# Start of a block feed-forward: filter transform ahead of the operands, first weight sums ahead of the norm, modulation rows spread out, a third residual row buffer

## The chip, the cores and the metric

One core of a Trainium2 chip runs the whole program. Its engines each work through their own list of instructions in order: PE (TensorE, matrix products), DVE (VectorE, elementwise work on two operands), ACT (ScalarE, copies, casts and functions), POOL (GpSimd, elementwise) and SP (SyncE, which here issues every transfer). An instruction that must wait for another engine waits on a semaphore, and everything behind it on its own engine waits with it. The metric is the time of one execution in device microseconds (us); the median over runs counts.

## What is computed

Two layers of a diffusion backbone over 512 latent and 256 context tokens of width 1024 (768 tokens, kept as columns). Layer 0 mixes with a gated DeltaNet and banded attention, layer 1 with retention and a Hyena convolution. Each layer ends in a modulated SwiGLU feed-forward. In the reference:

```
x = x + mod[2] * (o_lat.astype(x.dtype) @ w_out)
x = x + mod[5] * swiglu(modulate(rmsnorm(x, norm_ffn_w[layer]), mod[3], mod[4]),
                        ffn_w_in[layer], ffn_w_out[layer])
...
def swiglu(h, w_in, w_out):
    gate, up = jnp.split(h @ w_in, 2, axis=-1)
    return (jax.nn.silu(gate) * up) @ w_out
...
c_act = jax.nn.silu(c)
mod = jnp.split((c_act @ mod_w[layer] + mod_b[layer])[:, None], 6, axis=-1)
```

The context tokens have modulation values of their own (`mod_c`, from `c_ctx`), and the Hyena part needs the Fourier transform of its filters, which depends on the weights alone. Both are side work that this kernel fits in around layer 0's feed-forward.

## The kernel before

**The feed-forward of layer 0.** `block_ffn` computes gate and up of one hidden block of 128 channels together, as a 2 by 2 block product: the two halves are the halves of the 1024 input channels on one side and the two halves of 384 tokens on the other. Seven products do the work of eight. Each product is 12 matmuls of 128x384: four blocks of 128 input channels, and three terms for each (both numbers are split into a high and a low part: high by high, high by low, low by high). There are 22 hidden blocks ("pairs" of a gate and an up weight below, numbered from 0), worked through in groups of 4, 4, 4, 4, 3 and 3. After a group's hidden blocks, `group_out` multiplies them by the output weight for each of the 8 blocks `d` of 128 output channels and adds the product to a row of the residual: it loads the row `xr` (384 KB) from DRAM, adds on DVE, and stores it again.

**Operands.** Before the first product, `block_operands` makes the seven activations from the residual `xt` and the norm's statistics: 16 DVE instructions (SCALAR_TENSOR_TENSOR, with the statistics in PSUM) and as many ACT instructions apply scale and shift; then for each part an ACT cast gives the high part (`hx`, `x`, `t7h`) and a DVE subtraction the low part (`hx`, `x`, `t7l`), and further DVE additions and subtractions form the sums (tiles `hhi`, `hlo`, `hxt2`).

**Weights.** `weights(j)` inside `block_ffn` loads gate and up of a pair (two `wr` tiles of 512 KB), splits the gate tile by an ACT cast and a DVE subtraction (`wh`, `wl`; products 1 and 2), forms four sums on DVE (`us`, and one in place in `wr`) and splits five units (`uh` on ACT, `ul` on DVE; products 6, 7, 5, 4, 3 in this order).

**The side work.** `hy_freq` transforms the filters: 16 matmuls of `hs` by `F`, ACT copies `he` out of PSUM, and POOL adds and subtracts two at a time into `hab` (four tiles, two POOL instructions each), which SP stores to `hD`. It is written behind `block_operands`. `mod_rows` computes 56 blocks of modulation values on DVE, as a task in pieces: its first piece loads the vector `cb` (1 MB) and the first weight row `wm` (512 KB); its second applies silu to `cb` on ACT; and each piece from there on loads the next `wm` and runs one or two DVE instructions `wj` (the 24 blocks that the context needs have two). `K.bg(n, "mod")` runs n pieces where it stands; `BLOCK_MOD` says how many follow each hidden block, and `group_out` runs one for each `d`.

**What sets the order.** A scheduler reorders the program's instructions within each engine, and tiles come from pools that reuse memory. All transfers lie on one queue, SP's, and are issued in its order. `cb` lies in memory that `hab` had held, so its load waits for the last store of `hab`, on SP's queue and for the data.

```
BLOCK_MOD = (2,) * 6 + (1,) * 8 + (0,) * 8
...
            ops = K.block_operands(xt, st, saf, sbf, hp)
            K.hy_freq(*pf, 0, hsD, hD)
```

Of the kernel before, what the change touches and what calls it, by code (L numbers as in the profile page):

```python
# [10 lines left out]
F32R = mybir.dt.float32r  # L11
# [8 lines left out]
P = 128  # L20
D = 1024
KD = D // P
NL = 512
NC = 256
NT = NL + NC
# [9 lines left out]
FFN_GROUPS = (8, 7, 7)  # L35
BLOCK_GROUPS = (4, 4, 4, 4, 3, 3)
BLOCK_HID = 6
BLOCK_MOD = (2,) * 6 + (1,) * 8 + (0,) * 8
V_EARLY = (1,)
INV_PACE = (6, 6, 10, 5, 24)  # L40
SCAN_ORDER = "ssss" + "sa" * 7 + "as" + "aoaoaao"
# [110 lines left out]
class Kern:  # L152
# [1130 lines left out]
                split(n, k, xp[d + k][:, c:c + h])  # L1283
        return ops

    def block_ffn(self, l, ops, hp, hq, xr):
        K, A = self, self.A
        h = HT

        def unit(src, n=4):  # L1290
            hi, lo = (K.t(hq, (P, 4, P), "u" + x, F32R, bufs=6)[:, :n] for x in "hl")
            A.copy(out=hi, in_=src)  # L1292
            K.sub(lo, src, hi)
            return hi, lo

        def weights(j):
            g, u = (K.t(K.wp, (P, KD, P), "wr", bufs=3) for _ in range(2))
            K.dma(g, K.I["ffi"][l, j, 0])
            K.dma(u, K.I["ffi"][l, j, 1])
            hi, lo = (K.t(K.wp, (P, KD, P), n, F32R, bufs=2) for n in ("wh", "wl"))  # L1300
            A.copy(out=hi, in_=g)
            K.sub(lo, g, hi)
            S = K.t(hq, (P, 12, P), "us", bufs=1)
            s1, s2, s3 = S[:, :4], S[:, 4:8], S[:, 8:]
            K.add(s1, u[:, :4], u[:, 4:])
            K.sub(s2, s1, g[:, :4])
            K.sub(s3, g[:, :4], u[:, :4])
            K.sub(u[:, :4], g[:, 4:], s2)
            w = {1: (hi[:, :4], lo[:, :4]), 2: (hi[:, 4:], lo[:, 4:])}
            for m, src in ((6, s2), (7, s3), (5, s1), (4, u[:, 4:]), (3, u[:, :4])):  # L1310
                w[m] = unit(src)
            return w

        def product(ps, w, m, first=False):
# [5 lines left out]
        def hidden(j):  # L1320
            w = weights(j)
            x, y, z = K.mmps()[:, :h], K.wkps()[:, :h], K.wkps()[:, :h]
            f = K.t(hq, (P, 2 * h), "hf", bufs=2)
            a, b = (K.t(hq, (P, h), c, bufs=2) for c in ("ha", "hb"))
            product(x, w, 1, True)
            A.copy(out=f[:, :h], in_=x)
            product(y, w, 2, True)
            K.add(f[:, :h], y, f[:, :h])
            K.act(f[:, :h], f[:, :h], AF.Silu)
            product(x, w, 6)  # L1330
            A.copy(out=a, in_=x)
            product(z, w, 7, True)
            product(x, w, 5)
            A.copy(out=b, in_=x)
            K.add(b, z, b)
            product(z, w, 4)
            K.add(a, z, a)
            K.mul(f[:, :h], f[:, :h], a)
            product(x, w, 3)
            K.act(f[:, h:], x, AF.Silu)  # L1340
            K.mul(f[:, h:], f[:, h:], b)
            hi, lo = (K.t(hp, (P, NT), t, F32R, bufs=BLOCK_HID) for t in ("hhi", "hlo"))
            A.copy(out=hi, in_=f)
            K.sub(lo, f, hi)
            return hi, lo

        xt = None

        def group_out(g0, hs):
            nonlocal xt  # L1350
            nh = len(hs)
            last = g0 + nh == NH
            if last:
                xt = K.t(K.bp, (P, KD, NT), "x", bufs=1)
            for d in range(KD):
                raw = K.t(K.wp, (P, KD, P), "wr", bufs=3)[:, :nh]
                K.dma(raw, K.I["ffo"][l, d][:, g0:g0 + nh, :])
                w = unit(raw, nh)
                x = xt[:, d] if last else K.t(hq, (P, NT), "xr", bufs=2)
                K.dma(x, xr[d])  # L1360
                pl, pc = K.mmps(), K.wkps()
                K.proj_fm(w, ([t[0] for t in hs], [t[1] for t in hs]), K.halves(pl, pc))
                for p, c, r in K.parts(pl, pc):
                    K.stt(x[:, c], p, K.modc[l][:, 40 + d, r:r + 1], x[:, c])
                if not last:
                    K.dma(xr[d], x)
                K.bg(1, "mod")

        pend, start = [], 0
        for gn in BLOCK_GROUPS:  # L1370
# [448 lines left out]
def body(ctx, tc, I, out, dbg=None, stop=None):  # L1819
    K = Kern(ctx, tc, I, out, dbg)  # L1820
    K.setup()
    hD = K.t(K.dp, [2, 2, P, 2, 2, 512], "hD")
    hsD = K.t(K.dp, [2, 4, P, 2, 512], "hsD")
# [8 lines left out]
    with ExitStack() as s:  # L1832
        with ExitStack() as s2:
# [3 lines left out]
            xt = K.t(K.bp, (P, KD, NT), "x", bufs=1)  # L1837
# [16 lines left out]
        pf = K.pool(s, "hyf0")  # L1854
# [18 lines left out]
    with ExitStack() as s:  # L1873
        hp = K.pool(s, "hp")
        with ExitStack() as s2:
            K.sp = K.sx = K.pool(s2, "sp1", side="right")
            pf = [K.pool(s2, "hyf1a"), K.pool(s2, "hyf1b", side="right")]
            st = K.norm_stats(xt)
            for d in range(KD):
                K.dma(xr[d], xt[:, d])  # L1880
            ops = K.block_operands(xt, st, saf, sbf, hp)
            K.hy_freq(*pf, 0, hsD, hD)
        hq, mp = K.pool(s, "hq"), K.pool(s, "mp1", side="right")
        K.tasks["mod"] = [K.mod_rows(mp, [(0, n, True) for n in range(40, 48)] + [(1, n, n < 16) for n in range(48)])]
        xt = K.block_ffn(0, ops, hp, hq, xr)
    if stop == "l0":
        K.dma(dbg["x"], xt)
        return
# [41 lines left out]
```

## Time and profile before

| | |
|---|---|
| median of 3 runs | 1882.78 us (1876.31 to 1886.25) |
| the profiled execution | 1874.94 us |
| its span, first to last instruction | 1873.2 us |
| mean granted TensorE clock | 0.969 |
| PE busy | 1763.2 us, 94% of the span |
| DVE busy | 1192.3 us, 64% |
| ACT busy | 686.6 us, 37% |
| POOL busy | 105.7 us, 6% |

Times inside a run are counted from the start of the span. The granted clock is TensorE's, as a share of 2.4 GHz; 0.50 is its lower level, 1.2 GHz. An arrow `a <- b` behind "idle" or in a wait says that `a` stood still until `b` was done.

### The profile page before, as it was taken

What the parts mean: (1) busy time and instruction counts of PE and PEld (TensorE: products, weight loads), DVE (VectorE), ACT (ScalarE), POOL (GpSimd) and SP (SyncE); (2) the same over time, 40 slices, a digit from 0 to 9 for tenths busy, and PEclk for the clock granted to TensorE, in tenths of its full rate; (3) what the DMA queues carried; (4) which work ended last, traced back from release to release, by engine and by line L of the source; (5) the groups of instructions that cost most, each with busy time, mean ns of one, the idle gap of its engine ahead of it and who ended that gap; (6) DMA issues with size and microseconds to landing.
All of it is one profiled execution on the core that took longest, in us unless ns stands there. A gap on an engine that the chain in (4) does not pass through costs nothing.

```text
span 1873.2 us, 28543 instructions
## 1 busy us (share of the span) xinstructions
PE 1763.2 (94%) x11047; PEld 1596.8 (85%) x11047; DVE 1192.3 (64%) x2423; ACT 686.6 (37%) x1417; POOL 105.7 (6%) x94
## 2 busy tenths in 40 slices
PE   5999999999898399999999998999999999999999
PEld 4988899988696399999999997687998888888887
DVE  5686696458747799988765557668645663333333
ACT  2444444145615342433333323422442432222221
POOL 0011001100002300000000000200003100000000
PEclk9999999779899699999999998999999999999999
DMA  8344465445383447687744356422443523333332
GB/s 330 112 152 134 123 215 178 101 155 180 96 267 127 152 133 229 205 277 249 224 146 139 114 187 240 168 96 94 127 136 102 185 75 101 92 100 96 96 97 95
DMA packets 123076, 286.71 MB, mean 153 GB/s; under 512 B 28729, under 2 KB 45545, under 8 KB 119228
## 3 DMA queue, kind: packets, MB, share of 16 engines
q1 hardware_dynamic: 122940, 284.88, 46.5%
q8 instruction: 87, 1.43, 0.3%
q14 instruction: 49, 0.40, 0.1%
HBM read 228.96 MB, written 55.87 MB: 152 GB/s over the span
## 4 chain that ended last, share of the span: by engine, by line
PE 77%; DVE 10%; DMA 5%; ACT 3%; issue 3%; POOL 1%; SPq 0%; POOLq 0%; DVEq 0%; ACTq 0%
PE mm L193 52%; PE wk L193 23%; PE wk L197 1%; PE sa L193 1%; DVE wl L200 1%; POOL hab L200 1%; DVE ac L213 1%; DMA wm<-in_modt_dram 1%; ACT wh L250 1%; DMA xr<-xr 1%; PE sa L197 1%; DVE wj L213 0%; DMA rvt<-rvD 0%; DMA x<-in_xall_dram 0%; DMA vD<-tk 0%
## 5 line engine op out<-in xcount | busy, mean ns | idle before, releaser
L193 PE MATMUL mm<-hx,wh 128*128 128x512 f32 (+2 forms) x1968 | 524.3, 361 | 8.1 <-ACT hx L408 3.6
L193 PEld LDWEIGHTS mm<-hx,wh 128*128 128x128 f32 x1968 | 356.9, 190 | 52.0 <-ACT hx L408 3.8
L193 PE MATMUL mm<-hx,wl 128*128 128x512 f32 (+2 forms) x984 | 327.1, 360 | 0.8 <-DVE wl L200 0.8
L200 DVE TENSOR_TENSOR wl<-wr,wh 128x1024 fp32r<-128x1024 f32 (+1 forms) x159 | 193.3, 1216 | 190.5 <-ACT wh L250 179.1
L250 ACT CAST wh<-wr 128x1024 fp32r<-128x1024 f32 (+1 forms) x137 | 142.7, 1041 | 419.0 <-PE mm L193 414.0
L193 PE MATMUL mm<-wh,hx 128*128 128x256 f32 x1216 | 231.8, 290 | 2.6 <-DVE sv L963 1.1
L193 PEld LDWEIGHTS mm<-hx,wl 128*128 128x128 f32 x984 | 183.8, 190 | 24.0 <-issue 3.9
L193 PEld LDWEIGHTS mm<-wh,hx 128*128 128x128 f32 x1216 | 193.7, 195 | 5.5 <-issue 1.7
L193 PE MATMUL mm<-wl,hx 128*128 128x256 f32 x608 | 175.3, 289 | 0.0
L193 PE MATMUL mm<-hx,uh 128*128 128x384 f32 x352 | 90.4, 338 | 32.4 <-ACT uh L1292 32.4
L193 PEld LDWEIGHTS mm<-wl,hx 128*128 128x128 f32 x608 | 118.2, 195 | 1.0 <-issue 0.6
L213 DVE SCALAR_TENSOR_TENSOR wj<-wm,cb 128x1024 bf16<-128x1024 f32 x80 | 97.6, 1220 | 21.3 <-ACT cb L221 13.9
L1292 ACT CAST uh<-wr 128x512 fp32r<-128x512 f32 (+1 forms) x92 | 55.1, 602 | 148.5 <-PE wk L193 84.8
L213 DVE SCALAR_TENSOR_TENSOR x<-mm,modc,x 128x256 f32<-128x256 f32 (+3 forms) x72 | 40.7, 585 | 90.8 <-PE mm L193 88.6
L193 PEld LDWEIGHTS mm<-hx,uh 128*128 128x128 f32 x352 | 64.2, 190 | 32.8 <-ACT uh L1292 32.7
L200 DVE TENSOR_TENSOR ul<-wr,uh 128x512 fp32r<-128x512 f32 (+1 forms) x92 | 60.8, 664 | 20.4 <-ACT uh L1292 20.2
L193 PE MATMUL mm<-hhi,wh 128*128 128x512 f32 x176 | 68.5, 389 | 0.0
L193 PE MATMUL mm<-hhi,wl 128*128 128x512 f32 x176 | 68.5, 389 | 0.0
L193 PE MATMUL mm<-hlo,wh 128*128 128x512 f32 x176 | 68.5, 389 | 0.0
L1292 ACT CAST uh<-us 128x512 fp32r<-128x512 f32 x66 | 39.4, 620 | 77.4 <-DVE us L200 32.8
L200 DVE TENSOR_TENSOR hf<-hf,mm 128x512 f32<-128x512 f32 x22 | 15.1, 687 | 71.6 <-PE mm L193 71.6
L193 PE MATMUL mm<-hx,ul 128*128 128x384 f32 x176 | 59.3, 337 | 0.0
(438 smaller groups left out, 3441.9 us busy)
## 6 DMA issues: line engine op xcount, KB each, us to landing
wr<-in_ffi_dram SPq DMA_DIRECT2D x88, 512.0 KB
xr<-xr SPq DMA_DIRECT2D x80, 384.0 KB
wm<-in_modt_dram SPq DMA_DIRECT2D x56, 512.0 KB
wm<-in_modw_dram SPq DMA_DIRECT2D x20, 1024.0 KB
wr<-in_ffo_dram SPq DMA_DIRECT2D x32, 256.0 KB
wr<-in_rett_dram SPq DMA_DIRECT2D x16, 512.0 KB
wr<-in_ffo_dram SPq DMA_DIRECT2D x16, 448.0 KB
wr<-in_abf_dram SPq DMA_DIRECT2D x12, 512.0 KB
```

The lines of the kernel that those rows point to most:

```text
L193: self.T.matmul(out=out, lhsT=l, rhs=r, start=start, stop=stop, skip_group_check=True)
L197: self.T.transpose(out, in_, self.ident[:n, :n])
L200: (eng or self.V).tensor_tensor(out=out, in0=a, in1=b, op=op)
L213: self.V.scalar_tensor_tensor(out=out, in0=a, scalar=s, in1=b, op0=op0, op1=op1, **kw)
L250: self.A.copy(out=hi, in_=raw)
L1292: A.copy(out=hi, in_=src)
```

## The change

Four edits. `hy_freq` is written ahead of `block_operands`. The first pair's loads, its four sums and the split of four of its units are written ahead of the norm (`block_first`, `block_sums`), where products 6 and 7 take their weights from one cast of two units at once, and the sum for product 5 is copied into the gate's tile, so that only three casts `uh` are left for `weights(0)`. The modulation pieces are spread over all 22 hidden blocks, with one for every second `d` of `group_out`. The row `xr` has three buffers, and `ha` and `hb` one each where they had two.

```diff
-BLOCK_MOD = (2,) * 6 + (1,) * 8 + (0,) * 8
+BLOCK_MOD = (0, 1, 2, 2, 2, 2) + (1,) * 4 + (2,) * 12
+BLOCK_ROWS = 3
...
+    def block_sums(self, l, j, pool):
+        K = self
+        g, u = (K.t(K.wp, (P, KD, P), "wr", bufs=3) for _ in range(2))
+        K.dma(g, K.I["ffi"][l, j, 0])
+        K.dma(u, K.I["ffi"][l, j, 1])
+        hi, lo = (K.t(K.wp, (P, KD, P), n, F32R, bufs=2) for n in ("wh", "wl"))
+        K.A.copy(out=hi, in_=g)
+        K.sub(lo, g, hi)
+        S = K.t(pool, (P, 12, P), "us", bufs=1)
+        s2, s3, s1 = S[:, :4], S[:, 4:8], S[:, 8:]
+        K.add(s1, u[:, :4], u[:, 4:])
+        K.sub(s2, s1, g[:, :4])
+        K.sub(s3, g[:, :4], u[:, :4])
+        K.sub(u[:, :4], g[:, 4:], s2)
+        return {1: (hi[:, :4], lo[:, :4]), 2: (hi[:, 4:], lo[:, 4:])}, {6: s2, 7: s3, 5: s1, 4: u[:, 4:], 3: u[:, :4]}, S, g
+
+    def block_first(self, l, pool):
+        K = self
+        w, src, S, g = K.block_sums(l, 0, pool)
+        hi, lo = (K.t(K.wp, (P, KD, P), n, F32R, bufs=2) for n in ("wh", "wl"))
+        K.A.copy(out=hi, in_=S[:, :8])
+        K.sub(lo, S[:, :8], hi)
+        w[6], w[7] = ((hi[:, i:i + 4], lo[:, i:i + 4]) for i in (0, 4))
+        K.A.copy(out=g[:, :4], in_=src[5])
+        return w, {5: g[:, :4], 4: src[4], 3: src[3]}
+
...
         def weights(j):
-            g, u = (K.t(K.wp, (P, KD, P), "wr", bufs=3) for _ in range(2))
...
-            for m, src in ((6, s2), (7, s3), (5, s1), (4, u[:, 4:]), (3, u[:, :4])):
-                w[m] = unit(src)
+            w, src = K.block_sums(l, j, hq)[:2] if j else first
+            for m in (6, 7, 5, 4, 3):
+                if m in src:
+                    w[m] = unit(src[m])
             return w
...
-            a, b = (K.t(hq, (P, h), c, bufs=2) for c in ("ha", "hb"))
+            a, b = (K.t(hq, (P, h), c, bufs=1) for c in ("ha", "hb"))
...
-                x = xt[:, d] if last else K.t(hq, (P, NT), "xr", bufs=2)
+                x = xt[:, d] if last else K.t(hq, (P, NT), "xr", bufs=BLOCK_ROWS)
...
-                K.bg(1, "mod")
+                K.bg(d % 2, "mod")
...
+            first = K.block_first(0, K.sx)
             st = K.norm_stats(xt)
...
+            K.hy_freq(*pf, 0, hsD, hD)
             ops = K.block_operands(xt, st, saf, sbf, hp)
-            K.hy_freq(*pf, 0, hsD, hD)
```

The names in the rows below end in a number of the tile and one of its allocation. On ACT, at the start of the operands (`hhi`, `hlo`: scale and shift; `hx`: high parts; `he`: filter copies), before:

```order
L1500 COPY he_1037_6442<-wk_1039_6447 128x512
L221 ACTIVATE hlo_1014_6301<-hlo_1014_6301,modc0_9_87 128x512
L221 ACTIVATE hlo_1014_6301<-hlo_1014_6301,modc0_9_87 128x256
L1259 CAST hx_1017_6304<-hlo_1014_6301 128x384
L221 ACTIVATE hhi_1011_6298<-hhi_1011_6298,modc0_9_87 128x512
L221 ACTIVATE hhi_1011_6298<-hhi_1011_6298,modc0_9_87 128x256
L1259 CAST hx_1017_6304<-hhi_1011_6298 128x384
L1500 COPY he_1041_6455<-wk_1042_6456 128x512
```

and of the change, some rows earlier in the same stretch:

```order
L1516 COPY he_1029_6350<-wk_1031_6355 128x512
L222 ACTIVATE hlo_1042_6381<-hlo_1042_6381,modc0_9_87 128x512
L222 ACTIVATE hlo_1042_6381<-hlo_1042_6381,modc0_9_87 128x256
L1516 COPY he_1033_6363<-wk_1034_6364 128x512
L1260 CAST hx_1045_6384<-hlo_1042_6381 128x384
L222 ACTIVATE hhi_1039_6378<-hhi_1039_6378,modc0_9_87 128x512
L222 ACTIVATE hhi_1039_6378<-hhi_1039_6378,modc0_9_87 128x256
L1516 COPY he_1033_6363<-wk_1035_6368 128x512
L1260 CAST hx_1045_6384<-hhi_1039_6378 128x384
```

The last copy `he` of the four pairs (`he_1033` in the change) now stands in front of the fifth of the eight `hx` casts shown here; before (`he_1045`, not shown) it stood behind all eight, behind the eight `x` casts and behind two of the four `t7h` casts.

On ACT at the end of the operands (`cb`: silu of the modulation vector, `hf`, `ha`, `hb`: product results copied out of PSUM), before:

```order
L1326 COPY hf_1095_6674<-mm_1092_6671 128x384
L221 ACT_TABLE_LOAD
L221 ACTIVATE cb_1072_6627<-cb_1072_6627 128x2048
L1292 CAST uh_1054_6503<-us_1053_6498 128x512
L1292 CAST uh_1056_6507<-us_1053_6498 128x512
L1292 CAST uh_1058_6511<-us_1053_6498 128x512
```

and of the change:

```order
L1319 CAST uh_1056_6508<-wr_995_6230 128x512
L1319 CAST uh_1058_6512<-wr_996_6231 128x512
L1319 CAST uh_1060_6516<-wr_996_6231 128x512
L1260 CAST t7h_1049_6388<-hlo_1040_6379 128x384
L1342 COPY hf_1065_6523<-mm_1062_6520 128x384
L1293 CAST wh_1072_6628<-wr_1070_6624 128x1024
L222 ACT_TABLE_LOAD
L222 ACTIVATE cb_1093_6761<-cb_1093_6761 128x2048
L1347 COPY ha_1066_6524<-mm_1062_6520 128x384
```

The casts `uh` stood behind the silu of `cb` and now stand ahead of it; what stands behind it now is the copy `ha`, of the result of product 6.

On PE behind products 1 and 2 of pair 0 (operands `t7h`, `t7l` belong to product 7, `hx_1047` and `hx_1048` of the change to products 6 and 5), before:

```order
L193 MATMUL wk_1065_6524<-hx_1017_6304,wl_1052_6495 128x384
L193 MATMUL mm_1092_6671<-hx_1017_6304,wl_1080_6643 128x384
L193 MATMUL mm_1064_6523<-hx_1019_6306,uh_1054_6503 128x384
L193 MATMUL mm_1064_6523<-hx_1020_6307,uh_1054_6503 128x384
L193 MATMUL wk_1066_6525<-t7h_1021_6308,uh_1056_6507 128x384
```

and of the change, around the end of product 7:

```order
L194 MATMUL wk_1064_6522<-t7l_1050_6389,wh_1000_6243 128x384
L194 MATMUL wk_1064_6522<-t7h_1049_6388,wl_1001_6244 128x384
L194 MATMUL mm_1085_6657<-hx_1045_6384,wh_1072_6628 128x384
L194 MATMUL mm_1085_6657<-hx_1046_6385,wh_1072_6628 128x384
L194 MATMUL wk_1086_6658<-hx_1045_6384,wh_1072_6628 128x384
L194 MATMUL wk_1086_6658<-hx_1046_6385,wh_1072_6628 128x384
L194 MATMUL mm_1062_6520<-hx_1047_6386,uh_1056_6508 128x384
```

Before, the first matmul behind products 1 and 2 needs a unit `uh` that stands behind the silu of `cb` on ACT. In the change products 7 and 6 (24 matmuls, with weights `wh_1000` and `wl_1001` made ahead of the norm) come first, and the first matmul with an `uh` is that of product 5; it writes over the result that `ha` copies. Product 1 of pair 1 (`mm_1092` before), which ran ahead of the wait, is `mm_1085` and comes behind.

## Rows read from the trace of the kernel before

**Rows 1.** Costliest groups of the page: busy us, mean ns, idle before and releaser.

```profile
L193 PE MATMUL mm<-hx,uh 128*128 128x384 f32 x352 | 90.4, 338 | 32.4 <-ACT uh L1292 32.4
...
L250 ACT CAST wh<-wr 128x1024 fp32r<-128x1024 f32 (+1 forms) x137 | 142.7, 1041 | 419.0 <-PE mm L193 414.0
```

**Rows 2.** Windows: us, busy PE, PEld, DVE, ACT, POOL, granted clock, DMA share, GB/s.

```profile
605.05:637.41 32.36, 0.00 (x0) 0.00 (x0) 18.49 (x37) 12.19 (x24) 21.53 (x4) 0.58 0.29 120
637.41:640.80 3.39, 3.39 (x11) 3.15 (x12) 3.39 (x7) 2.46 (x5) 0.00 (x0) 0.52 0.43 171
640.80:651.77 10.97, 10.97 (x64) 10.67 (x63) 10.97 (x20) 5.10 (x9) 0.00 (x0) 1.00 0.53 160
```

**Rows 3.** Chain that ends at 642 us: start, us, what.

```profile
589.79 1.12 ACT hhi L221 x2
590.91 0.40 ACT hx L1259
...
594.16 0.48 ACT he L1500
...
601.99 9.80 POOL hab L200
...
622.43 4.16 POOL hab L200 x3
626.60 2.60 DMA hD<-hab
...
629.33 4.23 DMA cb<-in_crow_dram
...
633.65 1.28 ACT L221
634.94 1.91 ACT cb L221
```

**Rows 4.** POOL in order of time: start, us, instruction, idle before.

```profile
594.72 2.50 POOL L200 TENSOR_TENSOR hab<-he 128x512 f32<-128x512 f32 x2 [7.18 <-ACT he L1500]
601.99 24.59 POOL L200 TENSOR_TENSOR hab<-he 128x512 f32<-128x512 f32 x4 [4.76 <-issue]
```

**Rows 5.** DVE in order of time: start, us, instruction (rows between left out).

```profile
594.76 1.13 DVE L213 SCALAR_TENSOR_TENSOR hhi<-x,saffn,mm 128x512 f32<-128x512 f32 x2
596.10 1.54 DVE L200 TENSOR_TENSOR hx<-hlo,hx 128x384 fp32r<-128x384 f32 x1 [0.20 <-ACT hx L1259]
...
601.65 0.55 DVE L200 TENSOR_TENSOR hx<-hlo,hx 128x384 fp32r<-128x384 f32 x1
602.12 0.55 DVE L200 TENSOR_TENSOR hhi<-hhi 128x384 f32<-128x384 f32 x1
...
619.45 0.69 DVE L200 TENSOR_TENSOR us<-wr 128x512 f32<-128x512 f32 x1
...
621.26 0.55 DVE L200 TENSOR_TENSOR hf<-wk,hf 128x384 f32<-128x384 f32 x1
```

**Rows 6.** Waits from 640 to 1140 us: engine, line, what for, us, times, longest.

```profile
DVE xr L213 <- DMA xr<-xr: 18.8, 13, 3.6
DVE wj L213 <- DMA wm<-in_modt_dram: 7.2, 11, 1.4
PE wk L193 <- DVE hb L200: 5.1, 3, 2.7
PE mm L193 <- ACT hb L1334: 1.0, 1, 1.0
```

**Rows 7.** Tile wj from 640 to 1140 us (ns min/median/max, first and last start).

```profile
L213 DVE SCALAR_TENSOR_TENSOR wj<-wm,cb x79: 1214/1219/1227, 641.0 to 916.2; 128x1024 bf16<-128x1024 f32 x79
```

**Rows 8.** Windows in the feed-forward, columns as in group 2.

```profile
857.00:868.00 11.00, 8.31 (x41) 7.75 (x41) 9.99 (x18) 1.66 (x5) 0.00 (x0) 0.91 0.75 283
640.00:720.00 80.00, 80.00 (x455) 78.70 (x454) 79.26 (x137) 35.89 (x64) 0.00 (x0) 1.00 0.48 146
950.00:1150.00 200.00, 200.00 (x1141) 196.91 (x1139) 122.46 (x217) 71.86 (x121) 0.00 (x0) 1.00 0.47 154
```

More of the change, by code (lines that the diff above doesn't have):

```diff
@@ L1284, in block_operands, with block_ffn @@
         return ops
-    def block_ffn(self, l, ops, hp, hq, xr):
+    def block_sums(self, l, j, pool):
[22 more added lines that the diff above has]
+        return w, {5: g[:, :4], 4: src[4], 3: src[3]}
+    def block_ffn(self, l, first, ops, hp, hq, xr):
         K, A = self, self.A
@@ L1296, in weights @@
         def weights(j):
-            g, u = (K.t(K.wp, (P, KD, P), "wr", bufs=3) for _ in range(2))
[L1298 to L1309, printed above, removed]
-            for m, src in ((6, s2), (7, s3), (5, s1), (4, u[:, 4:]), (3, u[:, :4])):
-                w[m] = unit(src)
+            w, src = K.block_sums(l, j, hq)[:2] if j else first
+            for m in (6, 7, 5, 4, 3):
+                if m in src:
+                    w[m] = unit(src[m])
             return w
@@ L1880, in body @@
                 K.dma(xr[d], xt[:, d])
+            K.hy_freq(*pf, 0, hsD, hD)
             ops = K.block_operands(xt, st, saf, sbf, hp)
-            K.hy_freq(*pf, 0, hsD, hD)
         hq, mp = K.pool(s, "hq"), K.pool(s, "mp1", side="right")
         K.tasks["mod"] = [K.mod_rows(mp, [(0, n, True) for n in range(40, 48)] + [(1, n, n < 16) for n in range(48)])]
-        xt = K.block_ffn(0, ops, hp, hq, xr)
+        xt = K.block_ffn(0, first, ops, hp, hq, xr)
     if stop == "l0":
```

## The prediction

> **What bounds the kernel now.** The page says that PE is busy for 94% of the span, so only what PE waits for can be won without doing less on PE. The first view is the list of costliest groups: one group of matmuls, `mm<-hx,uh`, has 32.4 us of idle time ahead of it, put down to the ACT cast `uh` [rows 1]. The windows place it at 605.05 to 637.41 us, the start of the feed-forward: PE does nothing there, and the 11 matmuls behind it take 3.39 us at a granted clock of 0.52, where the next 64 take 10.97 us at 1.00 [rows 2]. So a matmul takes 0.17 us at full clock and a product of twelve 2.1 us; the low clock costs another 1.5 us.
>
> The chain of waits that ends there says why. ACT was not slow: `uh` stands behind the silu of `cb`, `cb` behind its transfer, that behind the store of `hab`, and that behind POOL [rows 3]. POOL is the surprise: four additions `hab` from 601.99 took 24.59 us, though the pair before took 2.50 for two [rows 4]. The last three of them take 4.16 us from 622.43, so the first took some 20.4 [rows 3, 4]. DVE's rows show beside what. From 601.65 it runs one subtraction after another, 0.47 us apart (the recorded 0.55 overlaps), all with both operands in SBUF, and the four `us` behind them; POOL got in only when `hf<-wk,hf` came at 621.26, whose operand lies in PSUM [rows 5]. In the stretch before, where DVE alternates with instructions that read PSUM, POOL's pair at 594.72 was not held up, and a DVE subtraction beside it took 1.54 [rows 4, 5].
>
> In the rest of the feed-forward PE loses 6.1 us to `hb`, in four waits, the longest 2.7 [rows 6]. In the window of that longest one PE is busy 8.31 of 11.00 us at a clock of 0.91, so about 1 us more is lost to the clock [rows 8].
>
> **The change part by part.**
>
> *Filter transform ahead of the operands.* POOL's last pair `hab` gets its input some 40 ACT instructions earlier: the order shows its last copy in front of the fifth `hx` cast. Operands start near 589; a part on ACT is 1.0 to 1.1 us for two shifts, 0.40 for its cast, 0.48 for a copy `he` [rows 3]. Four parts and five copies lie ahead: 4 x 1.5 + 5 x 0.48 + two shifts more = 9.5, so the last pair is ready at about 599, and the two before at 592 and 596. All three are then in the stretch where DVE still reads PSUM. At 1.25 us for one [rows 4] POOL would be through at about 602. DVE pays: 1.54 in place of 0.55 is 1.0 us [rows 5] for each pair, two more pairs than before, so 2.0. It saves the `us` at the end (below).
>
> *First weight sums ahead of the norm.* Products 6 and 7 need no `uh` any more, and the three casts left stand ahead of the silu. The time at which PE goes on comes from the operands. I take DVE's run of subtractions to start at 602.2 (16 with PSUM, in twos of 1.13 from 589 [rows 5], five subtractions at 0.47 between them and some 1.8 lost to POOL). There are 39 of them, to 620.5. Product 7's first low parts are through at about 613, so PE idles from 606 (products 1 and 2 of pair 0 only) to 613 and then does 24 matmuls, partly at the low clock of 0.3 us each, to 618.3. ACT meanwhile: last `t7h` cast at about 615, `hf` 0.48, `wh` 1.04 [rows 1], table load 1.28 and silu 1.91 [rows 3], to 619.6, then `ha` to 620.1. Product 5 may start then, and its low parts need the first `ul`, at 621.2; it ends at 623.2. `hb` is copied at 623.9, products 3 and 4 end at 628.1, and the 20 matmuls left of pair 1's products 1 and 2 at 631.6. Before, PE had done the same work at about 651.5 (the second window's 11 and the third's 64 matmuls are these five products and pair 1's product 2, and three more [rows 2]). That is 20 us, of which I give 1 back: pair 1's sums stand on DVE behind `hb`, and its load on SP behind `cb`, two `wm` and three rows. The load of `cb` no longer matters here: stored at 602.5, issued at 603 and landed at 607.3 (4.23 [rows 3]), some 9 us before ACT reaches it. Cover is gone only if `hab` ends behind 612.
>
> What moves ahead of the norm is the four sums on DVE (0.6 each [rows 5]), three ACT copies and casts of about 1 us [rows 1] and two DVE splits, into a stretch of the output projection. DVE's first sum waits there for a 512 KB load and stands ahead of an evacuation of PSUM. A transfer of this size took 2.60 us [rows 3]; bounds 0 and 3 us on PE, and I take 0, since the rows show no PE wait there now and PE runs one accumulation ahead.
>
> *Third residual row, modulation rows spread.* DVE waited 18.8 us for rows `xr` in 13 times, the longest 3.6, and 7.2 us for `wm` [rows 6]. `group_out` takes 24 matmuls for a row, 4.1 us. A buffer is in use for load, three additions and store: 384 KB at the rate of 512 KB in 2.60 [rows 3] is 2.0 each way, the additions some 1.6, and a wait of 3.6 on top gives 9.2, so 4.6 for a row on two buffers, longer than PE's 4.1, and 3.1 on three. Half as many `wj` in `group_out` (1.22 us each [rows 7], one or two to a piece) free DVE and the queue in the same place. Of 7.1 us idle and slow clock I take 5; bounds 0 and 7. The price is paid later: modulation ended at 917 [rows 7] and will now run to the last hidden block. From 950 DVE is busy 122 of 200 us and transfers run at 154 GB/s, where the window above had 283 [rows 8]. Some 40 `wj` and 18 MB more in that stretch make 171 us of 200 and 245 GB/s; I take nothing, the cover being those 29 us of DVE.
>
> One buffer of `ha` and `hb` and the moved loads of pair 1 cost nothing while DVE keeps up: both are read one product later.
>
> **Sum.** 19 + 5 = 24 us off the profiled 1874.94, so 1851; the median of the runs is 7.8 higher, 1882.78, and 24 off that is 1859. The three runs lie within 0.5%, and about 0.5%, 9 us, is what a measurement of this kernel can tell from no change.
>
> **Rivals.**
>
> *POOL is held up again* (0.20). The stretch with PSUM operands ends near 602, and the last pair gets its turn only if it is in by then. If its last addition is shut out, it waits for `hf<-wk`, which DVE now reaches at 622.3 (39 subtractions and three `ul`). `hab` ends at 623.6, `cb` is issued at 624.1 and lands at 628.4, silu 631.6, `ha` 632.1 against 620.1: 12 of the 19 us are lost, 7 + 5 = 12 remain, 1871. For it: the 20.4 us wait before was of just this kind [rows 4]. Against: the inputs are 3 us early. With two pairs shut out, 1875. The Trainium skill (SBUF — State Buffer, "Who interferes with whom") says that a DVE instruction with two SBUF inputs contends with a GpSimd instruction that reads SBUF, and that the one issued first holds the port for its whole instruction. By that alone POOL would wait for one subtraction at a time, half a microsecond, and this rival could not be; the measured wait ran through some 40 of them, so the row decides, and it stays in.
>
> *Let in at a gap* (0.12). A gap in DVE's run, where it waits for ACT's last `t7h` near 615, lets POOL through: `hab` at 617.5, `cb` at 622.1, silu 625.3, `ha` 5.7 later than above: 13 + 5 = 18, 1865.
>
> *Modulation rows put on PE's path* (0.05). In order on DVE a `wj` that waits for its `wm` holds `hb`, and PE with it. Before, such waits for `hb` came three times and cost up to 2.7 us [rows 6]. One in each of the hidden blocks 10 to 21 would be 12 x 2.7 = 32 us, so 1859 + 32 = 1891, slower than before. It decides from 24 / 12 = 2.0 us for each of these blocks, and speaks as slower by 0.5% from 2.8. Against: 154 GB/s and DVE at 61% there [rows 8].
>
> *The change does not do what it says* (0.08). The wait moves: the output projection stalls on the early sums by 3 us for several of its eight blocks, or pair 1 waits for its loads behind SP's queue as long as pair 0 did. Then 1876 to 1884.
>
> **How the numbers follow.** My forecast has 0.55. Its own range is 1852 to 1866: 5 us for the FFN bound of 0 upward, 3 for the early sums, and downward 2 of the FFN and a run spread of 5. The range for 8 in 10 reaches to the first rival and its single-run spread: 1847 to 1875. Faster by over 0.5% (below 1873.4): all of the forecast and the gap, 0.16 of the held-up rival, 0.01 of the last, 0.84. Slower (above 1892.2): 0.03 of the modulation rival and 0.01, 0.04. The rest, 0.12, is the same.
>
> **What would show it.** `hab` four times two at 1.25 to 2.5 us and over by 603; `cb` landed near 607 and silu waiting for nothing but its turn; PE's idle time split into some 7 us ahead of product 7 and a few around product 5, in place of 32; in 640 to 1140 few waits for `xr` and none for `hb` over 1 us; `wj` up to 1080 or so with no PE wait behind it. I am wrong if a `hab` of more than 10 us stands in the record, if the chain from `cb` to `uh` or `ha` is still there, or if the windows past 920 show PE idle.

## The result, and the profile after

The changed kernel takes 1854.38 us (median of 4 runs, 1849.36 to 1860.69); the kernel before, run four times beside it, 1884.26. The ratio is 0.9851, with a 95% interval of 0.9805 to 0.9897: 1.5% faster, clear of the noise. A second set of runs gave 1856.35 and 0.9871 (0.9839 to 0.9903). The profiled execution took 1851.05 us against 1874.94, 23.9 less. The forecast was 1859, 24 less than the median.

The answer to [rows 4] is POOL in order of time:

```profile
584.70 2.50 POOL L201 TENSOR_TENSOR hab<-he 128x512 f32<-128x512 f32 x2 [137.53 <-DVE nrst L214]
591.53 3.14 POOL L201 TENSOR_TENSOR hab<-he 128x512 f32<-128x512 f32 x2 [4.34 <-ACT he L1516]
595.41 2.52 POOL L201 TENSOR_TENSOR hab<-he 128x512 f32<-128x512 f32 x2 [0.73 <-POOL hab L201]
598.82 2.85 POOL L201 TENSOR_TENSOR hab<-he 128x512 f32<-128x512 f32 x2 [0.89 <-ACT he L1516]
```

All four pairs are through by 601.7; none takes longer than 3.14. DVE's rows show how narrow that was [rows 5]:

```profile
599.31 1.21 DVE L201 TENSOR_TENSOR hx<-hhi,hx 128x384 fp32r<-128x384 f32 x1
600.44 0.47 DVE L214 SCALAR_TENSOR_TENSOR hlo<-x,saffn,mm 128x256 f32<-128x256 f32 x1
600.84 1.24 DVE L201 TENSOR_TENSOR hhi<-hhi 128x384 f32<-128x384 f32 x1
602.00 0.55 DVE L201 TENSOR_TENSOR hx<-hhi,hx 128x384 fp32r<-128x384 f32 x1
```

The last instruction with an operand in PSUM stands at 600.44. A POOL addition ran beside each of the subtractions around it, and they took 1.21 and 1.24 us where an undisturbed one has 0.55. From 602.00 the run of subtractions is as dense as before.

PE's rows, cut to the places where it waits and starts the next product (idle time and its releaser in brackets), answer to [rows 2]:

```profile
600.58 0.45 PE L194 MATMUL mm<-hx,wh 128*128 128x384 f32 x1 [0.46 <-DVE hx L201]
...
602.60 0.45 PE L194 MATMUL wk<-hx,wh 128*128 128x384 f32 x1 [1.23 <-DVE hx L201]
...
611.78 0.69 PE L194 MATMUL wk<-t7h,wh 128*128 128x384 f32 x1 [5.36 <-ACT t7h L1260]
...
619.50 0.62 PE L194 MATMUL mm<-hx,uh 128*128 128x384 f32 x2 [0.65 <-ACT ha L1347]
...
623.15 0.62 PE L194 MATMUL mm<-x,uh 128*128 128x384 f32 x2 [0.59 <-ACT hb L1350]
...
630.91 0.33 PE L194 MATMUL wk<-t7h,uh 128*128 128x384 f32 x1
```

The one wait of 32.4 us for `uh` is gone. The longest left is 5.36, for the first part `t7h` of product 7. Windows of the two stretches that follow, in the columns of [rows 2]:

```profile
611.78:615.17 3.39, 3.39 (x9) 2.92 (x10) 3.39 (x9) 3.39 (x8) 0.00 (x0) 0.50 0.94 312
615.17:630.91 15.74, 14.07 (x76) 13.11 (x76) 15.74 (x30) 10.15 (x15) 0.00 (x0) 0.99 0.42 140
```

Nine matmuls ran at the lower clock behind that wait; the 76 behind them had the full one. ACT's silu of `cb` at 617.16 waits for nothing but its turn. It still stands ahead of the copy `ha`, and of PE's waits the 0.65 us ahead of product 5 are what is left of that chain.

In the rest of the feed-forward the waits have moved [rows 6]. The list of waits from 655 to 1090 us:

```profile
DVE xr L214 <- PE mm L194: 11.7, 11, 2.3
DVE wj L214 <- DMA wm<-in_modt_dram: 9.8, 11, 2.1
...
PE wk L194 <- DVE hb L201: 3.0, 4, 1.0
...
DVE xr L214 <- DMA xr<-xr: 0.8, 1, 0.8
```

DVE waited for a row's transfer 18.8 us in 13 times; it is now 0.8 in one (from 640 to 1140 too), and what DVE waits for most in adding the rows is PE itself. Its waits for `wm` grew from 7.2 to 9.8. PE's longest wait for `hb` fell from 2.7 to 1.0, and to 1.7 in the profile of the second set. The modulation rows, in the form of [rows 7], then windows in that of [rows 8]:

```profile
L214 DVE SCALAR_TENSOR_TENSOR wj<-wm,cb x80: 1216/1222/1241, 623.7 to 917.1; 128x1024 bf16<-128x1024 f32 x80
```

```profile
857.00:868.00 11.00, 10.74 (x62) 10.74 (x63) 10.75 (x20) 4.52 (x9) 0.00 (x0) 1.00 0.53 163
655.00:1090.00 435.00, 431.88 (x2461) 425.27 (x2460) 346.89 (x621) 153.03 (x260) 0.00 (x0) 1.00 0.61 199
```

The last `wj` is where it was, at 917 instead of 916, and not at 1080. Each engine runs its list in order, so it is the scheduler that moved forward the rows that the table places later, and "to the last hidden block" did not come about.

### The profile page after: what moved, and what is told of

Same layout as the page of the kernel before. It is cut to its first block, busy times and chain, and to the rows that moved or that the text cites. A ratio compares the mean times of both kernels' runs of the same rounds, so it can differ in the third digit from the quotient of the medians.

```text
span 1849.3 us, 28533 instructions
## 1 busy us (share of the span) xinstructions
PE 1765.9 (95%) x11047; PEld 1595.6 (86%) x11047; DVE 1192.7 (64%) x2422; ACT 689.4 (37%) x1417; POOL 87.1 (5%) x94
## 3 DMA queue, kind: packets, MB, share of 16 engines
q1 hardware_dynamic: 122940, 284.88, 47.1%
## 4 chain that ended last, share of the span: by engine, by line
PE 76%; DVE 13%; DMA 5%; ACT 3%; issue 3%; POOL 0%; SPq 0%; POOLq 0%; DVEq 0%; ACTq 0%
PE mm L194 51%; PE wk L194 23%; DMA wm<-in_modt_dram 2%; PE wk L198 1%; DVE wj L214 1%; PE sa L194 1%; DVE wl L201 1%; DVE ac L214 1%; ACT wh L251 1%; PE sa L198 1%; DVE ul L201 1%; DVE x L201 1%; DVE ivt L201 0%; DMA rvt<-rvD 0%; DVE ivy L201 0%
## 5 line engine op out<-in xcount | busy, mean ns | idle before, releaser
L194 PE MATMUL mm<-hlo,uh 128*128 128x384 f32 x176 | 58.9, 335 | 0.0
```

Of the source, the lines that this page charges most:

```text
L194: self.T.matmul(out=out, lhsT=l, rhs=r, start=start, stop=stop, skip_group_check=True)
```

## How the runs are compared

The profiled executions differ ahead of the change too. The first operand instruction on DVE starts anywhere from 584.46 to 595.02 us, with nearly the same work ahead of it (only the early sums differ). So each trace is also read from that instruction: how long until DVE splits the first and second hidden block (`hlo<-hf,hhi`), and how long until ACT's first square of the next layer's norm, where the feed-forward is over.

Each ratio is taken against runs of the kernel before in the same set, whose medians lie from 1880.80 to 1884.26; the four columns on the right come from one profile each.

| kernel | median us | ratio (95%) | first operand at | 1st block + | 2nd block + | end + |
|---|---|---|---|---|---|---|
| before | 1884.26 | | 589.01 | 64.6 | 77.5 | 543.9 |
| the change | 1854.38 | 0.9851 (0.9805 to 0.9897) | 588.67 | 42.4 | 56.3 | 519.8 |
| the change, second set | 1856.35 | 0.9871 (0.9839 to 0.9903) | 590.11 | 42.4 | 56.3 | 519.2 |
| transform_only | 1861.64 | 0.9891 (0.9867 to 0.9915) | 594.35 | 49.4 | 62.4 | 526.8 |
| sums_only | 1881.02 | 0.9998 (0.9979 to 1.0018) | 595.02 | 59.6 | 73.1 | 545.4 |
| one_operand_gaps | 1874.38 | 0.9968 (0.9950 to 0.9986) | 589.38 | 66.3 | 79.3 | 545.1 |
| odd_gaps | 1880.55 | 0.9979 (0.9957 to 1.0001) | 594.80 | 66.5 | 79.5 | 551.3 |
| psum_gaps | 1870.19 | 0.9944 (0.9915 to 0.9974) | 586.68 | 58.5 | 71.7 | 537.6 |
| pair1_ahead | 1857.98 | 0.9870 (0.9841 to 0.9899) | 591.33 | 47.1 | 60.5 | 525.7 |
| two_row_buffers | 1863.84 | 0.9901 (0.9869 to 0.9933) | 584.46 | 42.3 | 56.6 | 527.7 |
| old_table | 1864.75 | 0.9908 (0.9878 to 0.9938) | 594.43 | 41.2 | 57.9 | 529.6 |
| change_less_sums | 1862.45 | 0.9886 (0.9853 to 0.9920) | 589.95 | 50.1 | 62.9 | 531.8 |
| start_only | 1865.21 | 0.9924 (0.9898 to 0.9950) | 591.27 | 41.1 | 58.6 | 532.1 |

From the end of the feed-forward to the end of the program it is 740.3 us before and 740.8 after, so nothing is won or lost behind it.

## Experiments on the start

My theory: a POOL addition whose two operands lie in SBUF does not get its turn while DVE issues two-operand SBUF instructions back to back; it gets in when DVE idles or issues an instruction with an operand in PSUM. The rival: POOL was late for another reason, and the gain is that of the weight sums.

**Each of the two early moves by itself.** transform_only, on the kernel before:

```diff
-            ops = K.block_operands(xt, st, saf, sbf, hp)
             K.hy_freq(*pf, 0, hsD, hD)
+            ops = K.block_operands(xt, st, saf, sbf, hp)
```

> The kernel before with the filter transform alone written ahead of the operands; no early weight sums, old modulation table, two row buffers. My account (POOL's turn on the shared port is what held the first product units): the four pairs of additions are over by about 602, cb lands near 607, silu is over near 618; the weight sums still stand behind the operands on DVE (620 to 622), so the first unit cast is at about 621 and PE goes on at 622 to 623 instead of 637.4; the first unit product of pair 1 comes at about 637 instead of 651.8, and the time is 14 to 15 us below before. Rival (the early weight sums are what counts, and the transform's place alone only moves the wait): an idle stretch of about 30 us on PE again, pair 1's unit product within 3 us of 651, time within 0.3% of before.

sums_only takes the other half: `block_sums`, `block_first` and its call ahead of `norm_stats`, nothing else.

```diff
+            first = K.block_first(0, K.sx)
             st = K.norm_stats(xt)
...
-        xt = K.block_ffn(0, ops, hp, hq, xr)
+        xt = K.block_ffn(0, first, ops, hp, hq, xr)
```

> The kernel before with the first pair's loads, sums and four split units ahead of the norm; the transform stays behind the operands, old modulation table, two row buffers. My account (a POOL addition that is not in before DVE's run of two-operand subtractions is shut out until that run ends): one addition of 15 to 20 us again, let in at about 620 when DVE runs out of work that is ready; cb is issued near 624 and lands near 628.5, silu is over near 632, the three unit casts and product 5 come behind it, and pair 1's first unit product at about 643: 8 to 9 us below before in the profile. Rival (POOL only ever waits for the one DVE instruction in progress, half a microsecond): no addition longer than 3 us, the last one over by about 615, cb landed by 620, pair 1's first unit product at about 634, 17 us below before.

With the transform alone POOL's four pairs are as short as in the change (2.49, 3.14, 2.52, 2.85 us), PE's wait for `uh` falls from 32.4 to 16.4 and the first block comes 15.2 us sooner. The median is 20.1 us below before (16 to 25), more than the 14 to 15 that were expected and than the 17.1 of the trace at the end of the feed-forward. What is left of PE's wait ends with the casts `uh`, and these waited 4.17 us for the sums `us` on DVE after the silu was over:

```profile
621.33 1.91 ACT L221 ACTIVATE cb<-cb 128x2048 f32<-128x2048 f32 x1
627.41 1.66 ACT L1292 CAST uh<-us 128x512 fp32r<-128x512 f32 x3 [4.17 <-DVE us L200]
```

The sums are late because they stand on DVE behind all operands. This is the second wait in series, and the early sums remove it. Alone they change no time, and the 8 to 9 us that were expected of them did not come. POOL of sums_only, a piece of its chain of waits and its ACT rows show why:

```profile
608.01 22.32 POOL L201 TENSOR_TENSOR hab<-he 128x512 f32<-128x512 f32 x4 [4.77 <-issue]
```

```profile
608.01 9.80 POOL hab L201
617.81 8.83 issue
626.64 3.70 POOL hab L201 x3
```

```profile
634.79 1.91 ACT L222 ACTIVATE cb<-cb 128x2048 f32<-128x2048 f32 x1 [13.95 <-DMA cb<-in_crow_dram]
636.60 1.64 ACT L1319 CAST uh<-wr 128x512 fp32r<-128x512 f32 x3
638.15 0.47 ACT L1342 COPY hf<-mm 128x384 f32<-128x384 f32 x1
```

The long addition is back, though the sums are early. `cb` is issued at 628.41, ACT stands 13.95 us before its silu, and PE waits 16.3 us for the copy `hf`, which stands on ACT behind the silu and three casts. DVE's last subtraction started at 625.01 and is over at 625.55; the first of the last three additions starts at 626.64, one addition later. So POOL came in when DVE had nothing to do. In the trace the first block comes 5 us sooner and the feed-forward takes 6 us longer, which one profile can't put down to the edit (below); the time is that of before, 0.9998 (0.9979 to 1.0018). That the gain is the sums' own is thereby ruled out; why POOL was late is the question of the next runs.

**What lets POOL in.** Three kernels leave the transform where it was before and put eight more instructions into DVE's run, one behind each `t2` and each part of `xp`. They add work and remove none. one_operand_gaps multiplies a tile by 1.0 in place, so that the instruction has one operand in SBUF:

```diff
             K.sub(t2, b[:, h:], a[:, :h])
+            K.ts(t2, t2, 1.0)
...
             K.sub(xp[k][:, h:], xp[k + 4][:, h:], xp[k][:, h:])
+            K.ts(xp[k][:, h:], xp[k][:, h:], 1.0)
```

> The kernel before with eight extra DVE instructions that multiply a tile by 1.0 in place, one operand each, spread through the run of subtractions (four behind the sums for product 6, four behind those for product 7). Work is added, none is taken away. My account (POOL gets in as soon as DVE runs an instruction with one operand in SBUF): the two additions of the third pair get in at about 604 and 606 and those of the last pair at about 615 to 617, none longer than 4 us; cb lands near 625 instead of 633.6, DVE's run is 6 to 8 us longer, and PE goes on at about 629 instead of 637.4, so the time is about 8 us below before in spite of the added work. Rival (the long addition has another cause, such as POOL itself or its input): an addition of about 20 us again, the end of the additions at 626 or later, and the time that of before or up to 8 us above.

The expectation failed. POOL and the DVE rows:

```profile
602.37 26.74 POOL L200 TENSOR_TENSOR hab<-he 128x512 f32<-128x512 f32 x4 [4.77 <-issue]
```

```profile
605.58 0.54 DVE L200 TENSOR_TENSOR hx<-hxt,hx 128x384 fp32r<-128x384 f32 x1
606.04 0.34 DVE L217 TENSOR_SCALAR hxt<-hxt 128x384 f32<-128x384 f32 x1
606.31 0.55 DVE L200 TENSOR_TENSOR hhi<-hhi 128x384 f32<-128x384 f32 x1
```

POOL was shut out as before, and PE waited 34.5 us. The median is 0.32% below before all the same (0.9950 to 0.9986), though in the trace the first block comes 1.7 us later and the feed-forward ends 1.2 later: a difference of some 6 us in the medians can have a cause that no trace here shows. The multiplication moves its 384 columns in 0.27 us, from 606.04 to 606.31, where a subtraction takes 0.47. That haste is a hint, and no more, that it is no plain one-operand instruction. odd_gaps cuts it to 383 columns:

```diff
+            K.ts(t2[:, :h - 1], t2[:, :h - 1], 1.0)
...
+            K.ts(xp[k][:, h:NT - 1], xp[k][:, h:NT - 1], 1.0)
```

> The kernel before with the same eight one-operand multiplications, over 383 columns in place of 384. The earlier ones followed one another after 0.27 us, faster than the 0.47 of a subtraction of the same size, so they ran in a faster mode of DVE. Account A (that mode kept POOL out, and one operand in the ordinary mode lets it in): the multiplications take 0.47 us from one to the next, the additions get in at them, end by 617, and the time is 6 to 9 us below before. Account B (one operand in SBUF never lets POOL in here): an addition of over 20 us again, time at or above before. If they still follow after 0.27 us, the run tells nothing new.

It still takes 0.27 us and POOL's four additions 26.72, so this run says nothing new, and a one-operand instruction at the ordinary pace stays untried. psum_gaps has in the same eight places a subtraction of the same size whose second operand lies in PSUM, into a tile that nobody reads:

```diff
+            K.sub(K.t(K.sx, (P, h), "gap", bufs=1), t2, pl[:, :h])
...
+            K.sub(K.t(K.sx, (P, h), "gap", bufs=1), xp[k][:, h:], pl[:, :h])
```

> The kernel before with eight extra DVE subtractions into a spare tile, whose second operand lies in PSUM, spread through the run of subtractions as the one-operand ones were (four behind the sums for product 6, four behind those for product 7). The run with eight one-operand multiplications had left POOL's long addition at over 20 us. Account A (a DVE instruction with an operand in PSUM lets POOL in, as in the stretch before the run and at its end): the third pair's two additions go in at the first two gaps, near 605 and 607, the last pair's near 612 to 615, none longer than 5 us; the additions end by 617 instead of 626.6, cb lands near 625 and PE goes on at about 629 in place of 637.4 (times counted with the operands starting at 589), 6 to 9 us below before. Account B (POOL gets in only once DVE has run out of two-operand work, wherever the other operand lies): an addition of 20 us or more, and a time at or above that of before.

POOL and DVE:

```profile
599.66 4.77 POOL L200 TENSOR_TENSOR hab<-he 128x512 f32<-128x512 f32 x2 [4.76 <-issue]
607.85 2.95 POOL L200 TENSOR_TENSOR hab<-he 128x512 f32<-128x512 f32 x2 [3.41 <-issue]
```

```profile
601.20 0.55 DVE L200 TENSOR_TENSOR hx<-hlo,hx 128x384 fp32r<-128x384 f32 x1
601.67 0.54 DVE L200 TENSOR_TENSOR gap<-hxt,mm 128x384 f32<-128x384 f32 x1
602.14 1.18 DVE L200 TENSOR_TENSOR hx<-hxt,hx 128x384 fp32r<-128x384 f32 x1
603.24 1.61 DVE L200 TENSOR_TENSOR hhi<-hhi,hxt 128x384 f32<-128x384 f32 x1
...
608.05 0.54 DVE L200 TENSOR_TENSOR gap<-hxt,mm 128x384 f32<-128x384 f32 x1
608.58 1.10 DVE L200 TENSOR_TENSOR hx<-hxt,hx 128x384 fp32r<-128x384 f32 x1
```

DVE is never idle here: the rows follow each other at 0.47 us, but for those that are held up. Yet each pair is in at the first `gap` that it meets, and the two subtractions behind that `gap` are the ones held up (1.18 and 1.61, then 1.10 and 1.61). POOL's waiting fell from 20 us to some 2, PE's wait to 24.1, and the first block comes 6.1 us sooner. The median of this kernel with eight instructions more on DVE is 0.56% below before (0.9915 to 0.9974); with one_operand_gaps at 0.32% for no visible reason, it is the trace that carries the reading. That a subtraction with an operand in PSUM lets POOL in is shown. Why it does is not: it also has only one operand in SBUF, and no run separates the two.

The Trainium skill (SBUF — State Buffer, "Who interferes with whom") says that a DVE instruction with at most one SBUF input, outside the 2-port modes, does not contend with GpSimd, and that `tensor_scalar` can enter such a mode. The traces agree with both: `gap` lets POOL in, and the 0.27 us of the multiplication against 0.47 fits a faster mode, though no run here shows the mode itself. The same section says that whoever issues first has the shared ports for the whole instruction and that the other blocks. If that means a wait for one instruction, the traces show otherwise: POOL stood through some 40 of them.

**The wait that is left.** pair1_ahead fills PE's 5.4 us ahead of product 7: products 1 and 2 of pairs 0 and 1 and pair 1's gate load and split are written inside `block_operands`, in front of the sums of operands.

```diff
+        pre = [(K.block_pair(w, ops), None)]
+        g = K.block_gate(0, 1)
+        pre.append((K.block_pair({1: (g[1][:, :4], g[2][:, :4]), 2: (g[1][:, 4:], g[2][:, 4:])}, ops), g))
```

> The changed kernel with products 1 and 2 of pairs 0 and 1, and the split of pair 1's gate weights, written between the first operands and the sums, so that PE has 24 more matmuls (4.1 us) to do while it waits for product 7's operands. If that wait (5.4 us for t7h, and a slow clock behind it) is a cost of its own, it falls below 2 us, the first unit product of pair 1 comes 39 us behind the first operand instead of 42, and the time is 2 to 4 us below the changed kernel. Rival (DVE's run of subtractions sets the end whatever PE does in between): the one split more (1.2 us) in DVE's run delays product 5 by as much, and the time is that of the changed kernel.

The wait of 5.4 us is gone and nothing is won: 0.9870 where the change has 0.9871 in the same set. In the trace the first block even comes 4.7 us later, a loss that the medians, certain to some 6 us, do not show. The windows:

```profile
606.66:613.50 6.84, 5.90 (x16) 4.77 (x17) 6.84 (x14) 5.64 (x13) 0.00 (x0) 0.51 0.57 231
613.50:624.60 11.10, 8.10 (x40) 6.51 (x40) 11.00 (x24) 9.27 (x17) 0.00 (x0) 0.96 0.45 154
624.60:634.20 9.60, 9.03 (x27) 8.52 (x28) 6.73 (x12) 3.55 (x6) 0.00 (x0) 0.51 0.39 142
```

The matmuls of pair 1 that were brought forward ran partly at half clock (the 16 of the first window, some of them still pair 0's, in 5.90 us). So did the products of pair 0 that come later, 5 and most of 4 and 3: 27 matmuls in 9.03 us, where 27 at the full rate of 0.17 take 4.7. That alone is 4.3 us more; the first block comes 4.7 late. Small waits are spread over the whole stretch (the longest 1.3), and the clock is low in two stretches of it, where in the change eleven matmuls ran at the lower clock, two ahead of its one long wait and nine behind it.

## Experiments on the feed-forward

**Row buffers and table, one at a time, and neither.** In the change, two_row_buffers sets `BLOCK_ROWS = 2`:

> The changed kernel with two buffers for the residual row in place of three. My account (two buffers were too few for 4.1 us a row): DVE waits for rows from DRAM again, 15 us or more in some ten times between 620 and 1120, PE's waits for hb grow by 2 to 3 us, and the time is 2 to 4 us above the changed kernel. Rival (the few waits of PE in the feed-forward come from how its stages happen to meet, not from the row buffers): DVE waits for rows again, but PE's waits and the time stay within 1 us of the changed kernel in the profile.

old_table keeps three buffers and takes back the table and the call:

```diff
-BLOCK_MOD = (0, 1, 2, 2, 2, 2) + (1,) * 4 + (2,) * 12
+BLOCK_MOD = (2,) * 6 + (1,) * 8 + (0,) * 8
...
-                K.bg(d % 2, "mod")
+                K.bg(1, "mod")
```

> The changed kernel with the old modulation table and one piece for every d of the output projection. The changed kernel's modulation instructions were over at 917, as before, so the table moves only a few of them: away from the first two hidden blocks, and out of the output projections. Account A (the thinner rows are worth 1 to 3 us): DVE's first modulation instructions stand ahead of pair 1's sums, PE waits 1 to 3 us more between 620 and 660 or at hb, and the time is 1 to 3 us above the changed kernel. Account B (the table is worth nothing): PE's waits from 620 to 1120 within 1 us of the changed kernel's.

start_only takes back both, and the two buffers of `ha` and `hb` come back too:

> The changed kernel with the old modulation table, two row buffers and two buffers of ha and hb: what is left of the change is the start, the transform and the early sums. Undoing the row buffer alone had cost 8 us and the table alone 10 between the first operand and the end of the feed-forward (527.6 and 529.7 against 519.2 us). If the two costs add, this kernel takes some 537 there and its time is 16 to 18 above the changed kernel. If they hang together (three rows running ahead on the queue are what the old table's loads are late behind), the feed-forward loses what it lost before, 5 us more than the changed kernel, 524 to 525 us, and the time is 4 to 6 above. The first hidden block ends at 42 in both cases.

change_less_sums keeps both, and the transform, and takes back the early sums:

> The changed kernel without the early weight sums: transform ahead of the operands, new table, third row buffer, one buffer of ha and hb; pair 0's weights made like the others'. If the sums are worth 7 us on top of the early transform (the profile of the changed kernel and of the transform alone differ by that at the end of the first hidden block, 42.4 against 49.4 us behind the first operand) and nothing without it, the first hidden block ends at about 49.4 and the time is 6 to 8 us above the changed kernel, 17 to 18 below before. Rival (the sums were worth what they were worth alone, nothing): within 2 us of the changed kernel, 24 to 28 below before.

The last of these is read most easily. Without the early sums PE waits 16.4 us for `uh`, as in transform_only, and the first block comes at 50.1 us, as its first account has it; its median, 20.7 us below before, lies between the two accounts and decides nothing.

In the other three the first block comes where it does in the change (41.1 to 42.4 us), so these edits touch the feed-forward alone. With two buffers DVE waits for rows again, and PE for `hb` and `ha`; the waits from 655 to 1090 us:

```profile
DVE xr L214 <- DMA xr<-xr: 26.5, 17, 4.0
...
PE wk L194 <- DVE hb L201: 5.2, 3, 2.1
...
PE mm L194 <- ACT ha L1347: 3.3, 3, 1.8
```

With the old table DVE hardly waits for rows (0.5 us), and PE stands 5.80 us at one place, ahead of the first unit product behind a `group_out`, where the chain of waits reads:

```profile
730.55 5.60 DMA xr<-xr
...
738.67 6.49 DMA wm<-in_modt_dram
...
745.26 1.25 DVE wj L214 x2
...
747.76 0.68 DVE us L201 x2
...
749.66 0.63 ACT uh L1319
```

A `wm` waits on SP's queue behind rows, its `wj` holds the sums `us`, and PE waits for their cast. In the change's two traces the longest wait of PE from 655 to 1090 us is 1.0 and 1.7 us.

In the medians the five kernels that have the early transform but lack one or more of the other edits lie together, 1861.6 to 1865.2, whichever they lack; the change lies at 1854.4 and 1856.4. Within the set where they were run together, two_row_buffers and old_table are 7.5 and 8.4 us above the change, more than the 2 to 4 and 1 to 3 that were expected; their intervals overlap with its own, so a single difference is not certain. start_only fits neither of its accounts: it takes 532.1 us to the end of the feed-forward, between 525 and 537, and its median is 15.8 us below before, where the change's is 24.5. It reads as if the last 8 us come only with all edits at once: start_only has its first block 8 us before transform_only, and ends 5 us behind it. That is not shown, for 8 us is little more than the 6 of one_operand_gaps that have no visible cause. How much belongs to the buffer and how much to the table stays open, and the single buffers of `ha` and `hb` were never tried by themselves. From the second block to the end, one profile each, the unchanged feed-forward takes 464.4 us in transform_only, 466.4 in before, 472.3 in sums_only and 473.5 in start_only. The code is the same, and only its start differs, so differences of this size can't be put down to an edit. Nor is DVE's wait for rows the same as time lost: transform_only keeps it, 17.1 us in 13 times, and its stretch is only 1 us longer than that of the change (463.5 and 462.9).

## Why the prediction was right

**Filter transform.** Right in mechanism and in its times. POOL was through at 601.67 (forecast 602) and `cb` issued at 602.18 (603). psum_gaps shows what lets POOL in, and sums_only that without the early transform the long addition stays. The rival that POOL is held up again was a near thing: the last instruction with PSUM started 1.2 us before the last addition ended. The gap near 615, the second rival, did not arise, and did not matter.

**Weight sums.** Product 7 began at 611.78 (613), product 5 at 619.50 (620.1), pair 1's units at 630.91 (631.6). Against the first operand, the first block came 22.2 us sooner (64.6 - 42.4) and the second 21.2; the sum had 19. Of that, transform_only has 15.2 and the sums on top 7.0. The sum was some 2 us low; of it, 1 us had been given back for pair 1's sums and loads, and PE does not stand still for them before its units at 630.91. The price of 0 for the early sums in the output projection is not contradicted: PE's idle time ahead of the first operand is 47.1 to 49.0 us in the six traces without them and 47.2 to 50.4 in the seven with them, 0.9 more on average. The low clock behind the wait was there as priced (nine matmuls in 3.39 us).

**Feed-forward.** The term was 5 us. From the second block to the end it is 466.4 us before, 463.5 and 462.9 after: 2.9 and 3.5, so some 2 us less. Row buffers did what was said (18.8 us of waits to 0.8). What these edits are worth to PE stays open: transform_only has 464.4 without them, and start_only 473.5. The term was thought of as separable from the start; start_only speaks against that, but with one profile it does not show it.

**Modulation.** Wrong. I took the order in which the rows are written for the order in which they run, so the stretch from 950 on would carry some 40 `wj` and 245 GB/s. The scheduler moved them forward, the last one ran at 917, and the rival that rested on them, 32 us for PE, had no ground. PE was busy without a break from 950 to 1090, at 144 GB/s. The mistake cost the forecast nothing, since I had priced that stretch at nothing for another reason.

**The size.** 24 was the sum; the profiles differ by 23.9, the feed-forward's end by 24.1 and 24.7 from the first operand, the second set's medians by 24.5 (1880.80 to 1856.35). The first set's 29.9 has a wider interval, 0.9805 to 0.9897, which is 19 to 37 us. That the sum fits to a few tenths is luck: the start was worth 21 to 22 where it had 19, the feed-forward about 3 where it had 5, and the two errors cancel.

## What to carry to other kernels

Put POOL's two-operand SBUF work beside a stretch in which DVE reads PSUM; a POOL instruction that shows up at many times its usual length in a dense stretch of DVE is waiting and not working, and everything that waits for its result waits with it. When several waits lie in series ahead of one matmul, price them one by one but try them together: here the second fix was worth nothing without the first, and the medians suggest, without showing it, that the last 8 us need all four. Compare traces from an event that both share, since the stretch ahead can differ by ten microseconds between executions.

## What was not expected of the hardware

POOL was shut out for 17 to 21 us (an addition of 1.25 us took 18.7 in sums_only, 20.5 before and 22.6 in one_operand_gaps) by instructions that each last half a microsecond, and let in by one that reads PSUM, with DVE never idle. Filling PE's idle time with matmuls won nothing where it left small waits between them, at a granted clock of 0.51 in two stretches. And the same instructions ahead of the change ran at different clocks in different executions: from 100 to 150 us the granted clock was 0.99 in the trace of before and 0.91 in that of transform_only, from 500 to 550 it was 0.90 and 0.86; by the first operand they are 5.3 us apart. Over the whole stretch ahead of it the granted clock is 0.95 in the trace with the earliest first operand (584.46) and 0.93 in the four with the latest (594.35 to 595.02). What decides the clock there, no run here shows.
